# Operands of the first gate and up products split early, kept in DRAM and read back, in a one-core decoder trunk on Trainium2

## The chip, the cores and the metric

The kernel runs on 1 core of one Trainium2 chip. The metric is the device time of one execution in microseconds, taken as the median of 3 runs: 1397.15 us for the kernel before (1396.82 to 1398.56).

## The reference, cut to what matters

One layer (DEPTH = 1) over 1040 rows (1024 tokens behind 16 learned ones) of width 1024, in float32:

```python
u = rmsnorm(h, mix_norm_pre)
q, f_logit, i_in, g_out, v_pool, gate_a, gate_b = split(u @ w_in)
a = hgrn2(q, f_logit, i_in, g_out, ...)        # recurrence over chunks of 64 rows, 4 heads
p = multiscale_pool(v_pool, pool_proj, pool_scale)
z = sigmoid(gate_a) * (a @ w_branch_hgrn) + sigmoid(gate_b) * (p @ w_branch_pool)
h = h + rmsnorm(z @ w_out, mix_norm_post)
u = rmsnorm(h, ffn_norm_pre)
gt = causal_dwconv(u @ ffn_w_gate, conv_w, conv_b)          # 1024 -> 2816, three taps
y = (gelu(gt) * (u @ ffn_w_up)) @ ffn_w_down                # 2816 -> 1024
h = h + rmsnorm(y, ffn_norm_post)                           # returned without the 16 rows
```

## The kernel before

**Split products.** A float32 operand goes through TensorE as two parts of type fp32r. ScalarE (ACT) casts the raw tile `wraw` to its high part `whi`, and `wlo = wraw - whi` is the low part; each is a tile of 128 partitions x 1024 floats, 512 KB. A product is the sum of three chains of matmuls: high weights by high data, high by low, low by high (lines 262, 263 and 265 in a Strassen product, 160 to 162 and 172 to 174 elsewhere). `wsplit` (line 131) loads and splits one weight tile. Its subtraction stands on VectorE (DVE), or on GpSimd (POOL) for the tiles named in the table `POOLED`. `wraw`, `whi` and `wlo` have 3 buffers each, shared by all stages.

**Strassen units.** The gates of the mixer and the gate and up products of the MLP run as Strassen units of 256 output columns: seven products P1, P2, P6, P5, P3, P7, P4 instead of eight (class `Strassen`, line 179). P1, P2 and P4 take a block of the weights; P6, P5, P3 and P7 take sums of blocks, which POOL makes (lines 235 to 238). `ahead` (line 199) casts the operand on ACT (line 209) and subtracts on DVE (line 210), on POOL for the products 4 to 7 of the order. The data side is also split: P1 multiplies the quarter `b11` (tile `v`) of the normed rows, P2 `b21`, P3 `b22`, and P6, P5, P7 and P4 multiply sums of quarters, `t2`, `t1`, `t3` and `t4`. `put` adds a finished product in PSUM into the output (line 1197).

**The stages** in the order of time: values and pooling columns; the gate columns g; the mixer's gates, eight Strassen units that are each finished in two halves (100 to 262 us, the object `gates`); the stage that the string `ORDER` lists by hand (262 to 600 us): projections F (forget gates), Q, G, PV and PP by 128 columns each, among the steps `h0` to `h3` of the four heads, then the branch products BA and BB. A scheduler places the instructions there. Then the mix with `w_out` in three chunks of rows (600 to 716 us), and the **seam** from the mix to the MLP (716 to 796 us): the last chunk's three tiles of rows are added to the residual, normed (`own.norm`, lines 1106 to 1120), transposed on TensorE (line 1043) and combined into the quarters and their sums (`to_quarters`, lines 1046 to 1079). Eight products need only the first half of the rows, which was ready: P1 and P2 of gate units 0 to 3 (`EARLY` = 4). They stand among the transposes; the rest of gate unit 0 and then the whole of up unit 0 follow. From there on gate and up units alternate to 1196 us, and the down product ends the kernel.

In the seam and the mix the order of PE, ACT, DVE and POOL is the order of the code. SyncE (SP) issues loads and stores, in an order of its own; each waits for its buffer and for what it stores, and those behind wait with it.

**Names used below:** `tt` is a temporary of `to_quarters`; `un` a normed tile; `m` a tile of residual rows; `g` and `p` outputs and half sums of units; `pt` the transposes' bank; `swa`, `swb` the block sums; `st` a head's state; `d` and `kd` tables of a head.

Of the kernel before, what the change touches and what calls it, by code (L numbers as in the profile page):

```python
# [14 lines left out]
P = 128  # L15
# [19 lines left out]
HT = 514  # L35
# [8 lines left out]
ORDER = ("F0 c0 Q0 h0 F1 h0 c1 Q1 h0 h1 F2 h1 c2 h0 Q2 h1 h2 G2 h0 h1 h2 h0 F3 h0 h2 c3 PV0 h1 h2 h1 Q3 h3 h1 "  # L44
         "h3 h1 PV1 h3 sp0 PV2 h2 h3 sa1 sp1 sp2 PP0 h2 PV3 h2 h3 sp3 PP1 h0 G3 h3 PP2 h3 PP3 BB0 h2 BB1 BB2 "
         "sa2 BB3 h3 BB4 BB5 sa0 sa3 BA0 BA1 BB6 BA2 BB7 BA3 BA4 BA5 BA6 BA7")
# [10 lines left out]
def trunk_kernel(ctx: ExitStack, tc: tile.TileContext, x, meta_tokens, mix_norm_pre,  # L57
# [122 lines left out]
    class Strassen:  # L180
# [7 lines left out]
        def __init__(self, units, run, early, quarters, span, put, whole):  # L188
# [8 lines left out]
            self.got, self.at, self.prompt = [], 0, []  # L197

        def ahead(self, n):

            while len(self.got) < min(len(self.seq), self.at + n):
                i = len(self.got)
                if i % 2 == 0:
                    self.hi = wst.tile([P, 1024], F32R, tag="whi", name=nm("whi"))
                    self.lo = wst.tile([P, 1024], F32R, tag="wlo", name=nm("wlo"))
# [42 lines left out]
        def product(self, u, p, then=None):  # L248

            assert self.seq[self.at] == (u, p)  # L250
            x = pair(p)
# [4 lines left out]
            cuts = [(c0, o0, 512 - o0), (c0 + 512 - o0, 512, n - 512 + o0)][: 1 + (n + o0 > 512)]  # L256
            for k in range(4):
# [3 lines left out]
                for c, o, w in cuts:  # L261
                    pe.matmul(x[:, o : o + w], whi[:, k, :], xh[:, c : c + w], start=(k == 0), stop=False)  # L262
                    pe.matmul(x[:, o : o + w], whi[:, k, :], xl[:, c : c + w], start=False, stop=False)  # L263
                for c, o, w in cuts:
                    pe.matmul(x[:, o : o + w], wlo[:, k, :], xh[:, c : c + w], start=False, stop=(k == 3))  # L265
            x = x[:, o0 : o0 + n]
            if then and self.prompt:
                then(x)
                self.ahead(self.prompt.pop(0) - self.at)
                return x  # L270
            self.ahead(4)
            if then:
                then(x)
            return x
# [14 lines left out]
        def first(self, u):  # L289
# [3 lines left out]
            return (lambda: self.product(u, "P1", lambda x: act.copy(self.p1s[u], x)),  # L293
                    lambda: self.product(u, "P2", lambda x: self.put(u, 0, 0, self.p1s[u], x)))
# [7 lines left out]
        def rest(self, u):  # L302
            u2 = self.p1s[u]
            dve.tensor_tensor(u2, u2, self.product(u, "P6"), ALU.add)
            x5 = self.product(u, "P5")
            self.put(u, 0, 1, u2, x5, self.product(u, "P3"))
            self.whole(u, 0)
# [1190 lines left out]
```

## Time and profile before

| | us |
|---|---|
| median of 3 runs | 1397.15 |
| the profiled execution | 1396.61 |
| its span, first to last instruction | 1394.9 |
| PE busy | 1353.6 |
| DVE busy | 973.9 |
| ACT busy | 565.0 |
| POOL busy | 508.4 |

Some 1.7 us of the profiled execution lie outside the span. A stretch of the span is read with a row of the windows view: its length, the busy time of PE, PEld (weight loads), DVE, ACT and POOL, then the clock that TensorE was granted (1.00 is full), the share of the DMA engines and GB/s. The waits view lists idle time of an engine by the line that waited and the instruction that released it. Rows of the timeline give the start and the duration of one instruction or of a run of equal ones.

### The profile page before, as it was taken

What the parts mean: (1) busy time and instruction counts of PE and PEld (TensorE: products, weight loads), DVE (VectorE), ACT (ScalarE), POOL (GpSimd) and SP (SyncE); (2) the same over time, 40 slices, a digit from 0 to 9 for tenths busy, and PEclk for the clock granted to TensorE, in tenths of its full rate; (3) what the DMA queues carried; (4) which work ended last, traced back from release to release, by engine and by line L of the source; (5) the groups of instructions that cost most, each with busy time, mean ns of one, the idle gap of its engine ahead of it and who ended that gap; (6) DMA issues with size and microseconds to landing.
All of it is one profiled execution on the core that took longest, in us unless ns stands there. A gap on an engine that the chain in (4) does not pass through costs nothing. (4 is left out here: it accounts for less than half of the span.)

```text
span 1394.9 us, 21573 instructions
## 1 busy us (share of the span) xinstructions
PE 1353.6 (97%) x8405; PEld 1224.6 (88%) x8405; DVE 973.9 (70%) x1381; ACT 565.0 (41%) x945; POOL 508.4 (36%) x379
## 2 busy tenths in 40 slices
PE   8989999999999999999997999999999999999997
PEld 6879999999999899987777788888999988788786
DVE  6694655288975756565579888888887777654557
ACT  5443333356465463126564322222323223543343
POOL 4255331217543611051036565634567552000100
PEclk9999999999999999999998999999999999999999
DMA  6033433321111023589852577665677879966524
GB/s 245 31 100 121 138 104 108 103 73 46 33 33 33 18 76 122 182 265 316 288 172 91 148 218 214 192 173 145 161 166 188 197 194 268 365 231 201 179 71 166
DMA packets 133220, 215.21 MB, mean 154 GB/s; under 512 B 8327, under 2 KB 76523, under 8 KB 133120
## 3 DMA queue, kind: packets, MB, share of 16 engines
q1 hardware_dynamic: 121056, 189.47, 40.2%
q0 software_dynamic: 12064, 24.38, 10.3%
q8 instruction: 66, 1.08, 0.3%
q14 instruction: 34, 0.28, 0.1%
HBM read 160.84 MB, written 76.05 MB: 170 GB/s over the span
## 5 line engine op out<-in xcount | busy, mean ns | idle before, releaser
L262 PE MATMUL P<-v,whi 128*128 128x258 f32 (+2 forms) x528 | 162.6, 322 | 3.5 <-DVE g L1197 2.5
L263 PE MATMUL P<-v,whi 128*128 128x258 f32 (+2 forms) x528 | 161.6, 320 | 0.0
L265 PE MATMUL P<-v,wlo 128*128 128x258 f32 (+2 forms) x528 | 140.8, 321 | 1.1 <-DVE wlo L210 1.1
L137 POOL TENSOR_TENSOR wlo<-wraw,whi 128x1024 fp32r<-128x1024 f32 (+2 forms) x23 | 50.0, 2174 | 183.0 <-ACT whi L136 101.3
L262 PEld LDWEIGHTS P<-v,whi 128*128 128x128 f32 x528 | 100.8, 191 | 11.8 <-DVE g L1197 2.9
L263 PEld LDWEIGHTS P<-v,whi 128*128 128x128 f32 x528 | 100.7, 191 | 7.5
L161 PE MATMUL pd<-rot 128*128 128x512 f32 x272 | 106.0, 390 | 0.3 <-DVE rot L1257 0.3
L162 PE MATMUL pd<-rot 128*128 128x512 f32 x272 | 105.9, 389 | 0.0
L265 PEld LDWEIGHTS P<-v,wlo 128*128 128x128 f32 x528 | 87.9, 190 | 8.8 <-DVE wlo L210 1.3
L136 ACT CAST whi<-wraw 128x1024 fp32r<-128x1024 f32 (+2 forms) x44 | 36.2, 825 | 146.0 <-PE pba L174 31.3
L209 ACT CAST whi<-wraw 128x512 fp32r<-128x512 f32 x90 | 53.0, 617 | 101.8 <-PE P L263 83.9
L1257 DVE TENSOR_TENSOR rot<-yt,rot 128x1024 fp32r<-128x1024 f32 x33 | 41.2, 1250 | 71.0 <-ACT rot L1256 71.0
L210 DVE TENSOR_TENSOR wlo<-wraw,whi 128x512 fp32r<-128x512 f32 x82 | 75.9, 949 | 18.5 <-ACT whi L209 18.5
L1141 POOL TENSOR_TENSOR ys<-y 128x512 f32<-128x512 f32 x22 | 35.2, 1600 | 142.3 <-issue 96.8
L235 POOL TENSOR_TENSOR swa<-wraw,wraw 128x512 f32<-128x512 f32 x30 | 45.5, 1518 | 95.9 <-DMA wraw<-in_w_in_dram 62.4
L160 PE MATMUL pd<-rot 128*128 128x512 f32 x272 | 72.7, 390 | 2.0 <-ACT rot L1256 2.0
L1256 ACT CAST rot<-yt 128x1024 fp32r<-128x1024 f32 x33 | 34.6, 1053 | 90.2 <-PE pd L161 90.2
L209 ACT CAST whi<-swa 128x512 fp32r<-128x512 f32 x60 | 35.9, 619 | 86.8 <-PE P L263 71.6
L1189 DVE SCALAR_TENSOR_TENSOR y<-g,par,y 128x1024 f32<-128x1024 f32 x44 | 65.1, 1479 | 0.7
L160 PEld LDWEIGHTS pd<-rot 128*128 128x128 f32 x272 | 50.9, 188 | 13.5 <-ACT rot L1256 2.9
L210 DVE TENSOR_TENSOR wlo<-swb,whi 128x512 fp32r<-128x512 f32 x60 | 55.6, 932 | 9.7 <-ACT whi L209 9.4
L209 ACT CAST whi<-swb 128x512 fp32r<-128x512 f32 x60 | 35.9, 618 | 62.9 <-PE P L263 62.0
(344 smaller groups left out, 4320.2 us busy)
## 6 DMA issues: line engine op xcount, KB each, us to landing
wraw<-in_w_in_dram SPq DMA_DIRECT2D x36, 512.0 KB
yt<-ysum SPq DMA_DIRECT2D x33, 512.0 KB
wraw<-in_ffn_w_gate_dram SPq DMA_DIRECT2D x26, 512.0 KB
wraw<-in_w_out_dram SPq DMA_DIRECT2D x24, 512.0 KB
wraw<-in_ffn_w_up_dram SPq DMA_DIRECT2D x22, 512.0 KB
wsum<-in_ffn_w_down_dram SPq DMA_DIRECT2D x22, 512.0 KB
ysum<-ys SPq DMA_DIRECT2D x11, 768.0 KB
sa<-sscr SPq DMA_DIRECT2D x16, 513.0 KB
```

The lines of the kernel that those rows point to most:

```text
L137: eng.tensor_tensor(lo, raw, rr(hi), ALU.subtract)
L160: pe.matmul(ps, ahi, bhi, start=first, stop=False)
L161: pe.matmul(ps, ahi, blo, start=False, stop=False)
L162: pe.matmul(ps, alo, bhi, start=False, stop=last)
L209: act.copy(hi, src)
L210: (pool_e if 4 <= i < 2 * self.early else dve).tensor_tensor(lo, src, rr(hi), ALU.subtract)
L235: pool_e.tensor_tensor(s1, a21, a22, ALU.add)
L262: pe.matmul(x[:, o : o + w], whi[:, k, :], xh[:, c : c + w], start=(k == 0), stop=False)
L263: pe.matmul(x[:, o : o + w], whi[:, k, :], xl[:, c : c + w], start=False, stop=False)
L265: pe.matmul(x[:, o : o + w], wlo[:, k, :], xh[:, c : c + w], start=False, stop=(k == 3))
L1189: dve.scalar_tensor_tensor(a, g[:, :, j : j + n], cvw[:, j, m : m + 1], a, ALU.mult, ALU.add)
L1257: dve.tensor_tensor(lo, src, rr(hi), ALU.subtract)
```

## The change

Five things, all of one idea: operands that do not depend on data are split earlier, while PE works on the mixer's gates or on `ORDER`, and what was made lies in DRAM until it is wanted.

1. **Beside the gates.** After each half unit, `keep_next` runs one of 16 jobs: 12 make the low part of a weight tile of F, Q or PV (load, cast, subtraction, store of the low part), 4 split P1's and P2's operands of gate units 0 to 3 and store both parts. The stores are issued at the next call (`pay`).
2. **In `ORDER`.** The 12 loads of F, Q and PV read the raw tile and the kept low part (`wload`), and no longer subtract. Seven new steps `w4` and `w5` make the remaining five operands of gate unit 0 and the seven of up unit 0 (`keep_unit`), block sums included, on DVE and ACT, and store them.
3. **The first 20 products** of the MLP read ten pairs of kept tiles: no raw loads, block sums, casts or subtractions for them. Three tags of buffers take the pairs, and `lead` = 3 instead of `prompt` says how far ahead they are loaded.
4. **P2 onto P1.** `second` accumulates P2 in the bank in which P1's sum still stands, and ACT copies it to the output; before, `put` added it on DVE.
5. **The seam by hand.** `to_quarters` returns six steps, and the code calls them one by one among the products. The last chunk's `b22`, `t4` and `negdiff` go to DVE (argument `eng`); they stood on POOL.

The core of the diff:

```diff
-ORDER = ("F0 c0 Q0 h0 F1 h0 c1 Q1 h0 h1 F2 h1 c2 h0 Q2 h1 h2 G2 h0 h1 h2 h0 F3 h0 h2 c3 PV0 h1 h2 h1 Q3 h3 h1 "
+ORDER = ("F0 c0 Q0 h0 F1 h0 c1 Q1 h0 h1 F2 w4 h1 c2 h0 Q2 w4 h1 h2 G2 w4 h0 h1 h2 h0 F3 w5 h0 h2 c3 PV0 w5 h1 h2 h1 "
...
+                if i % 2 == 0 and i // 2 < len(self.kept):
+                    parts_, tags = self.kept[i // 2]
+                    both = [wst.tile([P, 1024], F32R, tag=t, name=nm(t), bufs=NRAW) for t in tags]
+                    for t, src in zip(both, parts_):
+                        self.loaded = nc.sync.dma_start(rr(t), src)
...
+            x = pair(p) if onto is None else onto
...
+    def keep(*what):
+        tiles_ = [wst.tile([P, 1024], F32R, tag=t, name=nm(t)) for t in ("whi", "wlo")]
...
+            if isinstance(src, tuple):
+                for a, op, b in src:
+                    dve.tensor_tensor(rr(lo), rr(lo) if a is None else a, rr(lo) if b is None else b, op)
+                src = rr(lo)
+            act.copy(hi, src)
+            dve.tensor_tensor(lo, src, rr(hi), ALU.subtract)
...
+    def keep_job(kind, i):
+        raw = wraw_tile()
+        nc.sync.dma_start(raw.rearrange("p (k c) -> p k c", k=KD), job(kind, i)[0])
+        hi, lo = (wst.tile([P, 1024], F32R, tag=t, name=nm(t)) for t in ("whi", "wlo"))
+        act.copy(hi, raw)
+        dve.tensor_tensor(lo, raw, rr(hi), ALU.subtract)
+        kept_w[kind, i] = dram.tile([P, 1024], F32, name=f"kept{kind}{i}")
+        owed.append((kept_w[kind, i], rr(lo)))
+
+    def wload(*key):
...
+        nc.sync.dma_start(rr(lo), kept_w[key])
+        act.copy(hi, raw)
...
+    def keep_next(u, i):
+        pay()
+        if beside:
+            beside.pop(0)()
...
-        put("b22", c22, d, pool_e)
-        put("t3", c12, d, dve)
-        negdiff(t2, t2, "b21", d)
-        return lambda: put("t4", t2, d, pool_e)
+        return [first_sums, lambda: put("t1", t1, d, dve), lambda: put("b22", c22, d, eng), difference,
+                lambda: negdiff(eng, t2, t2, "b21", d), lambda: put("t4", t2, d, eng)]
...
-        ffn.prompt = [5, 6, 8, 8, 8, 10, 10, 11]
...
+        ffn.lead, ffn.whole_pair = 3, True
...
+        todo.append(own.feat(0, dve))
+        second(0)
+        do(0)
...
+        first(3)
+        do(2)
+        do(1, 2)
+        second(2)
...
+        ffn.rest(RUN[0], dict(P6=[lambda: do(2, 3)]))
```

DVE in the seam, before: the queue from the last `un` on (L1120), with the sums of the three row tiles (`tt`; L1073, L1061, L1063) and the additions of finished P2s (`g`).

```order
L1120 SCALAR_TENSOR_TENSOR un_7222<-m_1008_7133,rstd_7226,g_790_6121 114x1024
L1197 TENSOR_TENSOR g_7254<-p_1015_7146,P_1031_7229 128x514
L1073 TENSOR_TENSOR tt_1041_7281<-tt_1043_7282,v_787_6117 128x456
L1073 TENSOR_TENSOR tt_1041_7281<-tt_1041_7281,v_787_6117 128x456
L1061 TENSOR_TENSOR tt_1041_7281<-tt_1043_7282,tt_1041_7281 128x456
L334 TENSOR_TENSOR t2l_6931<-tt_1041_7281,t2h_6929 128x2x114
L334 TENSOR_TENSOR t2l_6932<-tt_1041_7281,t2h_6930 128x2x114
L1063 TENSOR_TENSOR tt_1043_7282<-tt_1043_7282 128x456
L334 TENSOR_TENSOR v_788_6118<-tt_1041_7281,v_788_6118 128x4x114
L334 TENSOR_TENSOR t3l_6935<-tt_1043_7282,t3h_6933 128x2x114
L334 TENSOR_TENSOR t3l_6936<-tt_1043_7282,t3h_6934 128x2x114
L1197 TENSOR_TENSOR g_7328<-p_1015_7146,P_1044_7303 128x514
```

DVE at the same place now (the new L1232 is the old L1120, L1185 the old L1073, L1172 the old L1061, L348 the old L334):

```order
L1232 SCALAR_TENSOR_TENSOR un_7455<-m_1073_7377,rstd_7459,g_856_6365 114x1024
L1185 TENSOR_TENSOR tt_1094_7471<-tt_1096_7472,v_853_6361 128x456
L1185 TENSOR_TENSOR tt_1094_7471<-tt_1094_7471,v_853_6361 128x456
L1172 TENSOR_TENSOR tt_1094_7471<-tt_1096_7472,tt_1094_7471 128x456
L348 TENSOR_TENSOR t2l_7175<-tt_1094_7471,t2h_7173 128x2x114
L348 TENSOR_TENSOR t2l_7176<-tt_1094_7471,t2h_7174 128x2x114
L1185 TENSOR_TENSOR tt_1100_7517<-tt_1102_7518,v_853_6361 128x456
L1185 TENSOR_TENSOR tt_1100_7517<-tt_1100_7517,v_853_6361 128x456
L1172 TENSOR_TENSOR tt_1100_7517<-tt_1102_7518,tt_1100_7517 128x456
L348 TENSOR_TENSOR t2l_7175<-tt_1100_7517,t2h_7173 128x2x114
L348 TENSOR_TENSOR t2l_7176<-tt_1100_7517,t2h_7174 128x2x114
L348 TENSOR_TENSOR v_854_6362<-tt_1094_7471,v_854_6362 128x4x114
```

The additions into `g` are gone, and `t2` of the second row tile stands ahead of the first tile's `v`, `t1` and `t3`.

DVE in `ORDER`, after the tables `d` of head 1: before, one step follows the other there (L566 and L657 belong to the heads).

```order
L565 TENSOR_TENSOR d_3701<-d_3701,q_3636 128x130x4
L566 TENSOR_TENSOR d_3701<-d_3701,kk_3432 128x130x4
L657 COPY_PREDICATED sc_3023<-mbase,sb_3809 128x128 x4
L657 COPY_PREDICATED sc_3023<-mbase,sb_3818 128x128 x4
L660 COPY_PREDICATED scm_3024<-mbase,sm_3827 16x16
```

Now (the old L565 is L579, the old L657 is L671), with block sums (L845) and subtractions (L848) of step `w4` among them:

```order
L579 TENSOR_TENSOR d_3892<-d_3892,q_3815 128x130x4
L580 TENSOR_TENSOR d_3892<-d_3892,kk_3596 128x130x4
L845 TENSOR_TENSOR wlo_3820<-wraw_3606,wraw_3608 128x512
L845 TENSOR_TENSOR wlo_3820<-wraw_3606 128x512
L845 TENSOR_TENSOR wlo_3820<-wlo_3820,wraw_3606 128x512
L671 COPY_PREDICATED sc_3187<-mbase,sb_4006 128x128 x3
L845 TENSOR_TENSOR wlo_3820<-wraw_3608,wlo_3820 128x512
L671 COPY_PREDICATED sc_3187<-mbase,sb_4006 128x128
L671 COPY_PREDICATED sc_3187<-mbase,sb_4015 128x128 x4
L674 COPY_PREDICATED scm_3188<-mbase,sm_4024 16x16
```

Four block sums of 512 elements have come in between a head's tables and its selections.

SP in the gates, before: raw halves of the Strassen operands (L228) and stores of finished gates (`sscr`) alternate.

```order
L228 DMA wraw_1262<-in_w_in_dram 128x4x256
L777 DMA sscr<-sg_1224 128x514
L228 DMA wraw_1426<-in_w_in_dram 128x4x256
L777 DMA sscr<-sg_1255 128x514
L228 DMA wraw_1428<-in_w_in_dram 128x4x256
L779 DMA sscr<-sg_1356 128x512
```

Now, with the jobs' raw tiles (L896, 128x8x128) and the stores of what was kept (L862):

```order
L236 DMA wraw_1282<-in_w_in_dram 128x4x256
L791 DMA sscr<-sg_1244 128x514
L896 DMA wraw_1381<-in_w_in_dram 128x8x128
L791 DMA sscr<-sg_1275 128x514
L896 DMA wraw_1454<-in_w_in_dram 128x8x128
L793 DMA sscr<-sg_1376 128x512
L793 DMA sscr<-sg_1416 128x512
L862 DMA keptF_1387<-wlo_1384 128x1024
L236 DMA wraw_1461<-in_w_in_dram 128x4x256
L791 DMA sscr<-sg_1449 128x514
L236 DMA wraw_1463<-in_w_in_dram 128x4x256
```

Two jobs' raw tiles now stand ahead of the next unit's two halves in the three buffers of `wraw`, and a store of a low part ahead of them in the queue.

More of the change, by code (lines that the diff above doesn't have):

```diff
@@ L1273, in trunk_kernel @@
     last, t4s = None, []
+    assert ffn.seq[: len(KEPT)] == KEPT
+    ffn.kept = list(zip(kept, (("wraw", "wraw"), ("wraw", "wlo")) + (("whi", "wlo"),) * len(KEPT)))
     load_rows(0)
@@ L1304, in trunk_kernel @@
                 last = own
[L1306 to L1308 removed]
+        ffn.ahead(2)
         ws = [wo.next() for _ in range(3)]
```

195 lines of the change are left out of this document (133 added, 62 removed).

## The prediction

> **What bounds the kernel now.** I read the page's head first, then the windows by stage.
>
> ```profile
> PE 1353.6 (97%) x8405; PEld 1224.6 (88%) x8405; DVE 973.9 (70%) x1381; ACT 565.0 (41%) x945; POOL 508.4 (36%) x379
> 100.00:262.00 162.00, 159.63 (x1341) 159.63 (x1342) 80.73 (x115) 56.62 (x103) 55.66 (x41) 1.00 0.35 116
> 350.00:382.00 32.00, 30.68 (x251) 29.60 (x250) 31.89 (x70) 16.00 (x26) 18.01 (x7) 1.00 0.12 36
> 450.00:482.00 32.00, 29.50 (x226) 28.62 (x225) 28.91 (x38) 13.82 (x25) 18.94 (x8) 0.95 0.04 12
> 600.00:716.00 116.00, 112.85 (x526) 87.27 (x525) 70.57 (x91) 61.72 (x115) 27.29 (x23) 1.00 0.83 283
> 716.00:796.00 80.00, 65.99 (x423) 60.05 (x422) 71.68 (x85) 35.72 (x76) 46.10 (x37) 0.91 0.39 115
> 796.00:1196.00 400.00, 400.00 (x2473) 359.61 (x2471) 324.10 (x383) 116.80 (x181) 213.59 (x161) 1.00 0.75 197
> ```
>
> TensorE is busy for 1353.6 of 1394.9 us, so nothing is won except where it waits or runs slowly. One stage stands out: the seam, 716 to 796 us, with 14.0 us of idle PE, a clock of 0.91 and DVE busy for 71.68 of 80 us. The gates (100 to 262) have a full PE and a DVE half empty. In ORDER there are two stretches, 350 to 382 and 450 to 482, in which DVE is as good as full and PE already waits a little. After the seam PE is full for 400 us: what the seam gives is carried to the end.
>
> Next the waits of PE from 700 to 800, then the clock inside the seam:
>
> ```profile
> PE pt L1043 <- DVE g L1197: 6.2, 1, 6.2
> PE P L262 <- DVE g L1197: 2.9, 3, 1.8
> PE P L262 <- ACT t2h L333: 2.5, 1, 2.5
> PE P L265 <- DVE wlo L210: 1.1, 1, 1.1
> PE P L262 <- DVE p L308: 1.0, 1, 1.0
> 736.00:744.00 8.00, 1.80 (x14) 1.60 (x14) 8.00 (x7) 1.97 (x5) 7.89 (x6) 0.71 0.54 176
> 744.00:756.00 12.00, 9.53 (x60) 9.32 (x58) 10.89 (x15) 6.08 (x15) 4.93 (x4) 0.77 0.12 44
> 756.00:764.00 8.00, 7.91 (x51) 7.72 (x52) 7.98 (x11) 4.01 (x10) 6.32 (x5) 0.79 0.00 0
> ```
>
> DVE ends every large wait, directly or through the ACT cast of `t2h`. A mean clock of 0.71 over 8 us is 4.6 us at half, 0.77 over 12 is 5.5, 0.79 over 8 is 3.4: 13.5 us at half clock in all, of which some 4 us fall into the 6.2-us wait itself, so about 4.7 us of work are lost.
>
> How much is there at most? The first matmul of the seam, and the first of the second gate unit's P6, which ends it:
>
> ```profile
> 716.14 0.28 PE L262 MATMUL P<-v,whi 128*128 128x258 f32 x1
> L262 PE MATMUL P<-t2h,whi x8: 278/283/290, 796.0 to 798.4; 128*128 128x258 f32 x4, 128*128 128x256 f32 x4
> L265 PE MATMUL P<-t2h,wlo x8: 280/282/286, 796.4 to 798.7; 128*128 128x258 f32 x4, 128*128 128x256 f32 x4
> 787.61 0.39 PE L262 MATMUL P<-v,whi 128*128 128x512 f32 x1
> 790.39 0.40 PE L262 MATMUL P<-t3h,whi 128*128 128x512 f32 x1
> L1043 PE MATMUL pt<-ident,un 114*128 114x114 f32 x24 | 3.7, 308 | 6.2 <-DVE g L1197 6.2
> ```
>
> A gate product has 24 matmuls, the first at 796.0 and the last at 798.7: with one more start interval, 2.86 us. An up product (12 wide matmuls) starts 2.78 us after the one before it. Thirteen gate products, 24 transposes (at 0.1 us a start, 2.4 us) and seven up products are 37.2 + 2.4 + 19.5 = 59.1 us of work, and the stretch takes 79.8. **20.7 us** are lost there: 14.0 waiting, 4.7 by the clock, 2 at restarts. This is the ceiling of the change.
>
> **The seam, part by part.** What goes, and what the queue of DVE holds:
>
> ```profile
> L210 DVE TENSOR_TENSOR wlo<-wraw,whi 128x512 fp32r<-128x512 f32 x8 | 8.6, 1104 | 0.0
> L210 DVE TENSOR_TENSOR wlo<-swa,whi 128x512 fp32r<-128x512 f32 x6 | 6.1, 1030 | 0.1
> L1197 DVE TENSOR_TENSOR g<-p,P 128x514 f32<-128x514 f32 x7 | 4.7, 680 | 0.1
> 709.93 0.63 DVE L1063 TENSOR_TENSOR tt<-tt 128x456 f32<-128x456 f32 x1
> 710.47 0.63 DVE L334 TENSOR_TENSOR v<-tt,v 128x456 fp32r<-128x456 f32 x1
> 729.49 1.29 DVE L1120 SCALAR_TENSOR_TENSOR un<-m,rstd,g 114x1024 f32<-114x1024 f32 x1
> 736.96 1.69 DVE L1063 TENSOR_TENSOR tt<-tt 128x456 f32<-128x456 f32 x1
> ```
>
> Gone from DVE's queue are some 14 subtractions at 1.03 to 1.10 us and four additions at 0.68: about 17 of 71.7 us. Gone from POOL are the block sums of two units. Line 1063 stands there twice, the same operation: 0.63 us with POOL silent, 1.69 beside POOL's block sums. The moved `b22`, `t4` and `negdiff` put five 456-wide operations for each of three row tiles on DVE, at 0.54 us from start to start (709.93 to 710.47): 8 us. With POOL silent the operations that stay lose their extra 1.06 us, so DVE comes out well ahead.
>
> The new path: the order puts the eight early products and the three transposes one behind the other, 716.1 + 22.9 + 2.4 = 741.4 us for P6 of gate unit 0. P6 needs `t2` of the third row tile. The last `un` ended at 730.8 before; with the subtractions gone from among the norms I put its end at 728.7, an estimate. From there 19 operations at 0.54 us (two halves counted as one) stand to that `t2`: 10.3 us, and with 2 to 3 for their ACT casts 741 to 742. PE and DVE meet within half a microsecond, so 0.3 us of wait. P5, P3, P7 and P4 then have their data. Up's P1 needs the bank that P5's sum leaves, and its last addition stands on DVE behind three convolution operations of 1024 elements. Before, waits of this kind took 2.9 us in all and 1.8 at most; I take 2.6, between 0 and 5. With 0.3 for small ones: 20.7 − 3.2 = **17.5 us gained**, between 12 (one wait of 5 with its half clock) and 20.7.
>
> Whether 2.6 us idle also cost clock is read from a wait in ORDER:
>
> ```profile
> PE ppv L173 <- ACT st L667: 2.5, 1, 2.5
> 476.00:480.00 4.00, 2.94 (x10) 2.94 (x11) 4.00 (x7) 1.06 (x3) 0.00 (x0) 0.57 0.12 36
> 102.37 0.39 PE L262 MATMUL P<-uhi,whi 128*128 128x258 f32 x1 [2.66 <-ACT sg L714]
> 98.00:104.00 6.00, 3.34 (x24) 3.06 (x24) 4.51 (x15) 3.56 (x12) 3.73 (x5) 1.00 0.12 43
> ```
>
> A wait of 2.5 us was followed by 3.4 us at half clock, one of 2.66 us by none. So a wait of this length may cost 1.7 us more; that is in the range, not in the sum. The Trainium skill ("TensorE: Matmul & The Clock Gate", Part 1) has half rate only after an idle window of about 3.4 us: by it the sum stays at 1383.1, by the first row it would be 1384.8. The trace does not follow it in one of two cases.
>
> The ten pairs are 10.5 MB. A pair of 1.05 MB, at the 283 GB/s that the mix moved, takes 3.7 us, and two products take 5.7; loads go out two pairs ahead, so I cost them at nothing, with PE's products as cover. In SP's queue they stand behind the stores of residual rows, which wait for DVE until about 728; the pair behind them is wanted at 741.
>
> **Beside the gates.** Twelve jobs with one cast and one subtraction of 1024, four with two of each of 512, are some 20 us on DVE and 17 on ACT (prices below), where 81 and 105 us are free. Loads and stores add 18.9 MB in 162 us, 117 GB/s to 116; 283 was carried elsewhere. What it does cost is look-ahead: jobs take turns in the three `wraw`, so a unit's second raw half waits for the subtraction of the unit before. By the order, units 2 and 3 get P6's operands with under 1 us to spare, later ones with about 5. I take 1 us, between 0 and 6. Reading F's first low part back at the entry of ORDER passes SP's stores: 0.5 us, between 0 and 3.
>
> **In ORDER.** The rows for both sides, the same operation twice for each of two cases, and the page's groups:
>
> ```profile
> 352.66 3.40 POOL L137 TENSOR_TENSOR wlo<-wraw,whi 128x1024 fp32r<-128x1024 f32 x1
> 353.72 3.44 DVE L626 TENSOR_TENSOR kd<-kd,kk 128x1040 f32<-128x1040 f32 x1
> 373.80 1.23 DVE L626 TENSOR_TENSOR kd<-kd,kk 128x1040 f32<-128x1040 f32 x1
> 362.21 2.86 DVE L565 TENSOR_TENSOR d<-d,q 128x520 f32<-128x520 f32 x1
> 365.60 0.69 DVE L565 TENSOR_TENSOR d<-d,q 128x520 f32<-128x520 f32 x1
> 366.21 0.69 DVE L566 TENSOR_TENSOR d<-d,kk 128x520 f32<-128x520 f32 x1
> L136 ACT CAST whi<-wraw 128x1024 fp32r<-128x1024 f32 (+2 forms) x44 | 36.2, 825 | 146.0 <-PE pba L174 31.3
> 470.98 3.48 DVE L137 TENSOR_TENSOR wlo<-wraw,whi 128x1024 fp32r<-128x1024 f32 x1
> ```
>
> Seven steps add 26 operations of 512 on DVE, 0.61 us each (365.60 to 366.21): 15.9 us. Ten subtractions leave POOL. About 13 of the 26 fall into 350 to 382: +7.9 us, against 2.2 each for two operations that no longer run beside POOL's subtractions: +3.5 net in a stretch where PE has 1.3 us of idle. About 9 fall into 450 to 482: +5.5, but there the subtraction of 3.48 us that stands ahead of the state update (`st`, PE's 2.5-us wait) comes later in the new order. Together I take 2 us, between −4 (that wait and its half clock gone) and 8 (nothing hidden).
>
> **The sum.** −17.5 + 1 + 0.5 + 2 = −14.0 from the profiled 1396.61, 1382.6; the median stands 0.5 above the profiled execution, so **1383.1 us**.
>
> **The rivals.**
> - *DVE stays the bound of the seam.* For: 0.5 us decide at P6. If six of its operations run beside POOL or wait for ACT as at 736.96, P6 is 6.5 us late and loses 1.7 by the clock: gain 9.3, net −5.8, 1391.3. Against: POOL has no block sums before P6 in the new order. 0.15.
> - *Slower: the added DVE work starves PE in ORDER.* If the 22 operations in the two full stretches run at 1.69 us each, as beside POOL's heads' work, they are 37 us, of which the relief (4.4), PE's idle time there (3.8) and the subtraction that moves (3.5) cover 12: 25 us, and net −17.5 + 1.5 + 25 = +9, 1406. It turns the sign from 1.27 us an operation on. Against: POOL loses 10 subtractions. 0.14.
> - *Gates starve.* Eight units each late by 2 us: 16, net about 0 to +2, 1398. Against: about 5 us of slack in the later units. 0.05.
> - *Kept pairs arrive late.* SP's queue is in order; six pairs each 2 us late give 12 back: 1395. 0.06.
>
> **The numbers.** The forecast has 0.60. About 0.2% (2.8 us) is what a measurement can tell from no change. Faster: 0.60 + 0.15 + half of the last rival, 0.78; same: half of each of the last two, 0.06; slower: 0.14 and the rest, 0.16. The low end is a seam at its ceiling with gains in ORDER: 1374. The high end takes in the first and last rival: 1396.
>
> **What would show it.** Right: from the first P1 of the seam to the second gate unit's P6 about 62 us instead of 79.8, no 6.2-us wait at the transposes, a clock near 1.00, the largest wait at up's P1; PE in 100 to 262 idle for at most 4 us. Wrong: new waits of PE on `wlo` or on loads in the gates, DVE full from 350 to 382 with PE idle for over 4 us, or a wait at P6 of several microseconds.

## The result: 4.8 us slower, and the profile after

The changed kernel takes 1402.36 us (median of 20 runs, 1398.23 to 1406.59) against 1397.56 of the kernel before on the same chips: a ratio of 1.0034, 95% interval 1.0023 to 1.0045. The forecast was 1383.1, with 1396 as the end of its range. The profiled execution shown here took 1406.11 us, so it lies 3.7 us above the median, and the stages below add up to more than the medians differ by.

First the head of the changed kernel's page:

```profile
span 1404.3 us, 21770 instructions
...
PE 1356.8 (97%) x8405; PEld 1226.7 (87%) x8405; DVE 980.7 (70%) x1420; ACT 579.0 (41%) x961; POOL 455.8 (32%) x342
```

PE is busy for 3 us more in a span that is 9.4 us longer. The windows of the changed kernel follow (columns as before: PE, PEld, DVE, ACT, POOL busy, granted clock, DMA share, GB/s): the gates, the seam, which lies 23 us later here, and three windows around single waits.

```profile
100.00:262.00 162.00, 155.00 (x1277) 154.80 (x1278) 92.31 (x127) 68.64 (x116) 53.32 (x39) 0.98 0.64 202
739.00:805.00 66.00, 61.88 (x426) 57.06 (x425) 52.96 (x81) 28.16 (x63) 14.99 (x11) 0.97 0.71 237
167.00:181.00 14.00, 8.83 (x52) 8.63 (x51) 7.15 (x9) 5.62 (x9) 5.34 (x4) 0.76 0.76 233
269.00:285.00 16.00, 11.87 (x60) 11.13 (x59) 0.69 (x1) 4.49 (x6) 0.00 (x0) 0.79 1.03 329
482.00:494.00 12.00, 8.41 (x36) 7.54 (x36) 11.92 (x20) 8.41 (x12) 6.47 (x3) 0.72 0.46 158
```

The waits of PE in the changed kernel:

```profile
PE P L272 <- ACT whi L217: 5.2, 1, 5.2
PE ppp L173 <- DVE sc L671: 3.6, 1, 3.6
...
PE pq L173 <- ACT whi L908: 3.0, 1, 3.0
PE P L272 <- DVE p L321: 2.5, 1, 2.5
...
PE sm L673 <- ACT sg L728: 1.4, 1, 1.4
...
PE pf L173 <- ACT whi L908: 1.1, 1, 1.1
PE sb L668 <- DVE sc L615: 1.1, 1, 1.1
```

The 6.2-us wait of the seam is gone. Three new places took its room: one wait of 5.2 us in the gates, 3.0 and 1.1 at the entry of `ORDER`, and several inside it. The waits of 5.2, 3.0 and 3.6 us were each followed by half clock: means of 0.76 over 14 us, 0.79 over 16 and 0.72 over 12 in the last three windows are 6.7 us at half in each.

Where the lengths of stages come from, in the changed kernel: two rows of the timeline, the first product of the gates and of the seam,

```profile
101.83 0.39 PE L272 MATMUL P<-uhi,whi 128*128 128x258 f32 x1 [3.39 <-ACT sg L728]
...
738.89 0.28 PE L272 MATMUL P<-v,wraw 128*128 128x258 f32 x1
```

and the groups of F's, BB's and the second gate unit's P6's first chain, with the times of the first and the last:

```profile
L173 PE MATMUL pf<-uhi,whi x96: 316/322/658, 270.0 to 402.2; 128*128 128x346 f32 x64, 128*128 128x348 f32 x32
L173 PE MATMUL pbb<-phi,whi x96: 313/320/580, 534.2 to 599.4; 128*128 128x342 f32 x96
...
L272 PE MATMUL P<-t2h,whi x8: 277/283/287, 804.5 to 806.9; 128*128 128x258 f32 x4, 128*128 128x256 f32 x4
```

So the gates took 168.1 us from their first product, F to BB0 264.3, the seam 65.6 from its first product to P6. Before, read in the same way: 160.0, 250.5 and 79.8. The table has this in us for every kernel run (their names are explained with the experiments), each from one profiled execution, beside the median and the ratio of its runs to those of before on the same chip. What one execution can differ by is seen where code is the same: the gates of after, jobs_unused, w_late, w_act, w_thin and w_slot took 167.0 to 171.0 us, and ORDER took 264.3 in after and 270.1 in own_lo, 259.9 in jobs_unused and 265.5 in thin_store. Much of that is the clock. These two windows begin behind the same waits at `sb`, the first in jobs_unused, the second in thin_store:

```profile
373.00:390.00 17.00, 13.44 (x136) 12.37 (x135) 16.93 (x30) 13.16 (x22) 4.68 (x2) 1.00 0.39 137
...
375.00:392.00 17.00, 16.25 (x111) 15.15 (x112) 16.93 (x29) 13.21 (x22) 4.66 (x2) 0.50 0.39 133
```

In thin_store PE ran for 17 us at half clock there, in jobs_unused not at all, though the two waits before were 0.9 and 1.1 us in the one and 0.8 and 1.1 in the other. So a stage of one execution is better compared by PE's idle time, its length less PE's busy time, beside its length.

| kernel | gates | F to BB0 | BB0 to mix | mix | seam | median | ratio (95%) |
|---|---|---|---|---|---|---|---|
| before | 160.0 | 250.5 | 94.2 | 109.2 | 79.8 | 1397.6 | |
| after | 168.1 | 264.3 | 94.8 | 109.8 | 65.6 | 1402.4 | 1.0034 (1.0023 to 1.0045) |
| no_jobs | 168.8 | 259.2 | 94.8 | 112.0 | 62.1 | 1399.3 | 1.0017 (1.0006 to 1.0028) |
| own_lo | 163.6 | 270.1 | 94.8 | 109.0 | 62.6 | 1397.3 | 1.0006 (0.9991 to 1.0021) |
| first_first | 173.0 | 255.5 | 94.9 | 113.7 | 62.6 | 1399.8 | 1.0027 (1.0010 to 1.0043) |
| jobs_unused | 167.9 | 259.9 | 94.9 | 109.0 | 62.0 | 1397.8 | 1.0010 (0.9992 to 1.0027) |
| thin_store | 166.7 | 265.5 | 94.9 | 110.2 | 62.9 | 1399.2 | 1.0018 (1.0005 to 1.0031) |
| w_late | 169.7 | 250.0 | 101.5 | 110.5 | 62.9 | 1398.1 | 1.0005 (0.9992 to 1.0018) |
| w_act | 167.0 | 269.1 | 95.6 | 109.2 | 62.5 | 1402.9 | 1.0043 (1.0029 to 1.0057) |
| w_thin | 169.2 | 254.4 | 94.2 | 111.2 | 62.7 | 1394.8 | 0.9979 (0.9964 to 0.9993) |
| w_slot | 171.0 | 281.8 | 94.1 | 109.8 | 62.2 | 1423.6 | 1.0186 (1.0169 to 1.0204) |
| late | 160.0 | 250.5 | 108.8 | 109.7 | 62.8 | 1394.8 | 0.9978 (0.9968 to 0.9988) |
| late_u | 161.5 | 250.4 | 107.6 | 110.1 | 62.4 | 1394.6 | 0.9977 (0.9968 to 0.9986) |
| seam_pool | 160.0 | 249.9 | 108.6 | 109.2 | 62.5 | 1393.8 | 0.9973 (0.9964 to 0.9983) |
| mid_u | 160.1 | 248.3 | 99.8 | 109.7 | 63.0 | 1385.8 | 0.9926 (0.9912 to 0.9939) |
| mid_u2 | 162.7 | 249.8 | 99.7 | 111.1 | 62.1 | 1388.0 | 0.9933 (0.9919 to 0.9946) |

### The profile page after: what moved, and what is told of

Its sections match the earlier page's. It is cut to its first block, busy times and chain, and to the rows that moved or that the text cites. A ratio compares the mean times of both kernels' runs of the same rounds, so it can differ in the third digit from the quotient of the medians.

```text
span 1404.3 us, 21770 instructions
## 1 busy us (share of the span) xinstructions
PE 1356.8 (97%) x8405; PEld 1226.7 (87%) x8405; DVE 980.7 (70%) x1420; ACT 579.0 (41%) x961; POOL 455.8 (32%) x342
## 5 line engine op out<-in xcount | busy, mean ns | idle before, releaser
L272 PE MATMUL P<-v,whi 128*128 128x258 f32 (+1 forms) x496 | 153.6, 323 | 4.1 <-DVE p L321 2.5
L273 PE MATMUL P<-v,whi 128*128 128x258 f32 (+1 forms) x496 | 153.2, 323 | 0.0
L275 PE MATMUL P<-v,wlo 128*128 128x256 f32 (+2 forms) x512 | 137.6, 322 | 0.0
L272 PEld LDWEIGHTS P<-v,whi 128*128 128x128 f32 x496 | 94.1, 190 | 12.8 <-DVE p L321 2.9
L273 PEld LDWEIGHTS P<-v,whi 128*128 128x128 f32 x496 | 94.0, 190 | 7.8
L275 PEld LDWEIGHTS P<-v,wlo 128*128 128x128 f32 x512 | 85.0, 189 | 7.7
L217 ACT CAST whi<-wraw 128x512 fp32r<-128x512 f32 x78 | 46.1, 618 | 97.0 <-PE P L273 80.0
L218 DVE TENSOR_TENSOR wlo<-swa,whi 128x512 fp32r<-128x512 f32 x56 | 51.2, 923 | 20.2 <-ACT whi L217 6.7
L160 PEld LDWEIGHTS pd<-rot 128*128 128x128 f32 x272 | 50.8, 188 | 14.0 <-ACT rot L1369 2.3
L272 PE MATMUL P<-t2h,whi 128*128 128x258 f32 (+1 forms) x196 | 57.4, 310 | 5.2 <-ACT whi L217 5.2
L161 PEld LDWEIGHTS pd<-rot 128*128 128x128 f32 x272 | 51.1, 188 | 11.3 <-DVE rot L1370 0.7
L162 PEld LDWEIGHTS pd<-rot 128*128 128x128 f32 x272 | 51.1, 188 | 10.6
```

The costliest lines, as they stand in the source:

```text
L160: pe.matmul(ps, ahi, bhi, start=first, stop=False)
L161: pe.matmul(ps, ahi, blo, start=False, stop=False)
L162: pe.matmul(ps, alo, bhi, start=False, stop=last)
L217: act.copy(hi, src)
L218: (pool_e if 4 <= i < 2 * self.early else dve).tensor_tensor(lo, src, rr(hi), ALU.subtract)
L272: pe.matmul(d, whi[:, k, :], xh[:, c : c + w], start=(k == 0 and onto is None), stop=False, **go)
```

## The experiments

### Where the gates lose

Without the twelve jobs for F, Q and PV (`no_jobs`; the four jobs of the MLP then take the first four half units):

```diff
-    beside = [lambda o=o_: keep_job(*o) for o_ in order if o_[0] in ("F", "Q", "PV")]
-    beside += [lambda e=e: keep_first(e) for e in range(EARLY)]
+    beside = [lambda e=e: keep_first(e) for e in range(EARLY)]
```

> The changed kernel without the twelve jobs for F, Q and PV beside the gates; ORDER loads and splits these tiles as before, and the steps w4 and w5 stay in ORDER. Theory A (tiles that are held until their stores have landed, and raw loads queued behind them, starve PE in the gates and at the entry of ORDER): the gates take 160 to 161 us again from their first product to F's first matmul (168.1 in the changed kernel), the waits on whi at F and Q go, and the time is 1402.4 - 8 - 7 = about 1387 us. Theory B (the work that was added on DVE inside ORDER is the loss): the gates hardly change what the end sees, and with POOL's subtractions back the stage F to BB0 is longer than the changed kernel's 264 us; about 1402 or more.

Measured 1399.3 us. The entry's waits went, as theory A had it, but the gates' wait stayed, at 5.5 us: a miss. So the number and the kind of the jobs do not explain it: the four cost as much here as all sixteen did.

Low parts of the twelve jobs in buffers of their own (`own_lo`):

```diff
-        hi, lo = (wst.tile([P, 1024], F32R, tag=t, name=nm(t)) for t in ("whi", "wlo"))
+        hi, lo = wst.tile([P, 1024], F32R, tag="whi", name=nm("whi")), slot(1024, F32R, "klo")
```

> The changed kernel, but the low parts that the twelve jobs make lie in buffers of their own instead of the three of wlo. Theory A: the wait of 5.2 us in the gates (a subtraction that waited for a low part's store to land) goes with its half clock, gates 160 to 162 us; at the entry the buffers of the last four jobs are still held, so its 7 us stay: about 1394. Rival (the raw loads are late by the DMA traffic itself, not by the buffers): gates remain at 166 to 168 us, about 1402.

Measured 1397.3, not 1394. The wait fell to 1.8 us and the gates to 163.6; the entry's loss stayed. What the low parts' buffers did to this stays open: in this execution PE also ran at half clock from 102.9 us on (0.61 over 102 to 106), so it came to unit 3 later, and P6 started there 69.2 us after the gates' first product, where the six profiled executions with the changed kernel's gates have 68.4 to 71.6; the 163.6 itself lies below their 167.0 to 171.0. Last, whole stores against stores of 8 columns, with ORDER splitting for itself in both (`jobs_unused`, `thin_store`):

```diff
-    loader = Loader([o_ if o_ in kept_w else job(*o_)[:2] + (P, eng("w%s%d" % o_)) for o_ in order if o_[0].isupper()],
+    loader = Loader([job(*o_)[:2] + (P, eng("w%s%d" % o_)) for o_ in order if o_[0].isupper()],
...
-        owed.append((kept_w[kind, i], rr(lo)))
+        owed.append((kept_w[kind, i], rr(lo)[:, :8]))      # thin_store alone
```

> The changed kernel with its sixteen jobs beside the gates, but ORDER splits F, Q and PV itself as before and reads no kept low part. Gates as in the changed kernel, 167 to 173 us with a wait of 3 to 5 us in the third unit. Reading the low parts back should be worth 1 to 4 us in ORDER, so F to BB0 is 1 to 4 us longer here than the changed kernel's 264.3: 1403 to 1406.

> As the kernel whose low parts are made and not used, but the twelve jobs store 8 columns of the low part instead of 1024. If low parts held until their stores have landed are the gates' loss, the wait in the third unit falls below 1 us and the gates take 160 to 163 us; the total falls by 5 to 8 against the kernel with whole stores. If the raw tiles that the jobs load (a third of wraw, and ahead of the unit's own halves in SP's queue) are the loss, the gates stay at 167 us or more.

The wait on `whi` was 2.5 us with whole stores and 1.2 with thin ones, but the gates took 167.9 and 166.7 us: other waits, on `sg` and `p`, took the room (2.5 us with whole stores, 3.7 with thin ones). The total did not fall, and the first expectation, 1403 to 1406, was missed from below; why is told with the entry. So the landing of the low parts' stores is at most a small part. The trace shows the larger one: when POOL starts the block sums of the mixer's units 2 and 3 (unit 3 is the one that my expectations call the third). POOL's timeline before:

```profile
134.47 1.29 POOL L235 TENSOR_TENSOR swa<-wraw,wraw 128x512 f32<-128x512 f32 x1 [5.27 <-DMA wraw<-in_w_in_dram]
...
147.59 1.31 POOL L235 TENSOR_TENSOR swa<-wraw,wraw 128x512 f32<-128x512 f32 x1 [7.62 <-DMA wraw<-in_w_in_dram]
```

The same two in the changed kernel:

```profile
147.85 1.29 POOL L243 TENSOR_TENSOR swa<-wraw,wraw 128x512 f32<-128x512 f32 x1 [19.30 <-DMA wraw<-in_w_in_dram]
...
167.40 1.29 POOL L243 TENSOR_TENSOR swa<-wraw,wraw 128x512 f32<-128x512 f32 x1 [13.92 <-DMA wraw<-in_w_in_dram]
```

And in `mid_u`, a kernel told of below, in which no job stands in the early half units:

```profile
131.97 1.30 POOL L242 TENSOR_TENSOR swa<-wraw,wraw 128x512 f32<-128x512 f32 x1 [3.87 <-DMA wraw<-in_w_in_dram]
...
146.09 1.32 POOL L242 TENSOR_TENSOR swa<-wraw,wraw 128x512 f32<-128x512 f32 x1 [8.94 <-DMA wraw<-in_w_in_dram]
```

Units 2 and 3 had their sums started at 134.5 and 147.6 us before, at 147.9 and 167.4 after, and unit 3's P6 was due at 167.8. The queue of SP in the changed kernel says why:

```profile
127.46 0.37 SPq L896 DMA_DIRECT2D wraw<-in_w_in_dram  x1
128.55 0.38 SPq L896 DMA_DIRECT2D wraw<-in_w_in_dram  x1
...
139.43 0.41 SPq L236 DMA_DIRECT2D wraw<-in_w_in_dram  x1
...
156.22 0.41 SPq L236 DMA_DIRECT2D wraw<-in_w_in_dram  x1
...
162.81 0.38 SPq L236 DMA_DIRECT2D wraw<-in_w_in_dram  x1
163.24 0.50 SPq L862 DMA_DIRECT2D keptQ<-wlo  x1
```

And DVE's timeline:

```profile
170.05 1.63 DVE L218 TENSOR_TENSOR wlo<-swa,whi 128x512 fp32r<-128x512 f32 x1 [4.49 <-DMA keptQ<-wlo]
```

The two buffers that came free at 127 us went to jobs (L896), where before unit 2's halves stood. The look-ahead fell back by a whole unit and never came back: unit 3's second half left at 162.81, and POOL could start at 167.40. At the same time DVE waited 4.5 us for `keptQ`, 6.8 us after its issue. That is not what PE's wait of 5.2 us ended with: P6 began at 172.96, behind the cast of its sum on ACT, and ACT's timeline shows what stood ahead of that cast.

```profile
171.34 1.04 ACT L898 CAST whi<-wraw 128x1024 fp32r<-128x1024 f32 x1 [1.46 <-DMA wraw<-in_w_in_dram]
172.29 0.61 ACT L217 CAST whi<-swa 128x512 fp32r<-128x512 f32 x1
```

POOL had the sum ready at 171.1; ACT was waiting for a job's raw tile and then cast it first, which cost 1.2 us more. That the place is what counts is shown by `no_jobs` and `mid_u`: the same four jobs cost 8.8 us in the first four half units (gates 168.8) and 0.1 us from the sixth on (160.1; 162.7 in `mid_u2` with the same gates, 161.5 in `late_u` without any job there).

### Where the entry of ORDER loses

In the changed kernel the last jobs store both parts. ACT's timeline at the entry, with what its casts for F and Q waited for:

```profile
272.98 1.04 ACT L908 CAST whi<-wraw 128x1024 fp32r<-128x1024 f32 x1 [2.65 <-DMA kept3h<-whi]
...
276.04 1.04 ACT L908 CAST whi<-wraw 128x1024 fp32r<-128x1024 f32 x1 [1.48 <-DMA wraw<-in_w_in_dram]
```

The first of the two stood behind the store of `kept3h`, which still held its `whi`. `first_first` turns the order of the jobs round:

```diff
-    beside = [lambda o=o_: keep_job(*o) for o_ in order if o_[0] in ("F", "Q", "PV")]
-    beside += [lambda e=e: keep_first(e) for e in range(EARLY)]
+    beside = [lambda e=e: keep_first(e) for e in range(EARLY)]
+    beside += [lambda o=o_: keep_job(*o) for o_ in order if o_[0] in ("F", "Q", "PV")]
```

> The changed kernel with the sixteen jobs beside the gates in another order: the four that store both parts come first, the twelve of F, Q and PV after them. If F's cast at the entry of ORDER waited for a high part whose store had not landed (the last job before it stored both), the waits of 3.0 and 1.1 us at pq and pf go, and from F's first matmul to BB0 it takes 257 to 259 us instead of 264.3: 1395 to 1397 in all. If any job at the end of the gates does this, it stays at 262 to 265. The wait of 5 us in the third gate unit should stay, as it did without the twelve jobs.

F to BB0 took 255.5 us, without a wait at `pq` or `pf`: the entry is settled. The total, 1399.8, missed its 1395 to 1397: the gates took 173.0 with the wait of 5.4 us, and the mix 113.7. The same numbers say what the kept low parts are worth: 255.5 with them, 259.2 and 259.9 where ORDER subtracted for itself with the same steps `w4`, `w5` and no wait on casts at the entry (`no_jobs`, `jobs_unused`). That is some 4 us, of which 2.1 and 2.8 are idle PE (7.0 against 9.1 and 9.8) and the rest clock. (`thin_store`, with the same ORDER as these two, had 7.9 us of idle PE and its 17 us at half clock: 265.5.) The entry took back 7 us in the changed kernel's profiled execution, 4.1 of them waits; in `w_late` and `w_thin`, which have the same entry, it came down to 2.3 and 2.2 us of waits and no half clock. `jobs_unused`, which throws the jobs' work away and pays next to nothing of this, came out at 1397.8, below the changed kernel and against its expectation.

### Where ORDER loses

The steps `w4` and `w5` moved behind PP3, among BB and BA (`w_late`):

```diff
-... F2 w4 h1 c2 h0 Q2 w4 h1 h2 G2 w4 h0 h1 h2 h0 F3 w5 ... PV0 w5 ... PV1 w5 ... PV2 w5 ...
+... BB3 h3 w4 BB4 w4 BB5 w4 sa0 sa3 BA0 BA1 BB6 w5 BA2 w5 BB7 w5 BA3 w5 BA4 BA5 BA6 BA7
```

> The changed kernel with its seven steps w4 and w5 moved behind PP3, among BB and BA; the twelve jobs stay beside the gates. Theory A: only the 6.8 us that were lost inside ORDER after its entry can go, the gates keep their 168 us and the entry its 7 us: 1395 to 1397 us. Theory B: the same 6.8 us go, and nothing else is left to explain, so the time should fall below before's 1397.6 by most of the seam's 14 us: about 1384. A third case: the stalls inside ORDER come from low parts that are read back late; then they stay and the time remains near 1402.

F to BB0 fell to 250.0 us, the waits inside ORDER to those of before, and the gates kept their loss. The total came to 1398.1 and not 1395 to 1397, because BB0 to the mix grew to 101.5. So the loss inside ORDER comes with the steps; but is it the length of their operations, or the buffers that they wait for? Two kernels asked. In `w_act` ACT copies raw blocks into both parts, and DVE has none of the 26 operations, so the MLP's first products go without block sums and low parts:

```diff
-            if isinstance(src, tuple):
-                for a, op, b in src:
-                    dve.tensor_tensor(rr(lo), rr(lo) if a is None else a, rr(lo) if b is None else b, op)
-                src = rr(lo)
+            if at[0] >= 2 * EARLY:
+                src = src[0][0] if isinstance(src, tuple) else src
+                act.copy(hi, src)
+                act.copy(lo, src)
+                continue
```

> The changed kernel, but the seven steps w4 and w5 in ORDER make no sums and no subtractions: ACT copies a raw block into both parts (two casts where there was one, and 26 DVE operations less). The values of the MLP's first products are therefore not the reference's; its time is read for ORDER alone. Theory B (DVE's 26 operations delay the heads): from F's first matmul to BB0 the 264.3 us shrink by 7 to 9, and PE's waits between 370 and 385 us and the one of 3.6 us at ppp fall back to those of before (1.1 and 2.5 us); about 1394 us. Theory A (the buffers that the steps hold until their stores land): the stage stays at 262 to 265 us, about 1402.

In `w_thin` the 26 operations stay where they are in DVE's queue, 8 columns wide. The casts read raw blocks instead of the sums, and the high part is stored a second time in the low part's place:

```diff
-                    dve.tensor_tensor(rr(lo), rr(lo) if a is None else a, rr(lo) if b is None else b, op)
+                    dve.tensor_tensor(rr(lo)[:, :1, :8], a[:, :1, :8], b[:, :1, :8], op)
...
+                dve.tensor_tensor(lo[:, :1, :8], src[:, :1, :8], rr(hi)[:, :1, :8], ALU.subtract)
...
+            tiles_[1] = tiles_[0]
```

> The changed kernel, but the 26 operations that the steps w4 and w5 put on DVE work on 8 columns instead of 512, in the same places of the queue; the high part is stored in place of the low one and is a raw block, so the first MLP products are not the reference's. If the time of the DVE operations is ORDER's loss, F to BB0 shrinks from 264.3 to about 257 (7 us of entry wait stay), the waits at sb, sc and ppp fall to before's: 1395. If the waits for buffers in DVE's queue are the loss, it stays at 262 to 265: 1402.

PE's longest wait from F to BB0 in `w_act`:

```profile
PE ppv L173 <- ACT st L681: 6.5, 1, 6.5
```

And of `w_thin`:

```profile
PE ppv L173 <- ACT st L681: 2.7, 1, 2.7
PE pq L173 <- ACT whi L916: 1.4, 1, 1.4
```

`w_thin` answers it: the stage fell to 254.4 us, the waits at `sb` and `ppp` are gone (what is left is before's wait at `ppv`, the entry's and small ones), and 1394.8 us is what was expected of the operations' length. DVE's own waits for buffers stayed, as two rows of `w_thin` show,

```profile
433.60 0.24 DVE L846 TENSOR_TENSOR wlo<-wraw,wraw 128x8 f32<-128x8 f32 x2 [2.81 <-PE pq L177]
...
473.06 0.17 DVE L846 TENSOR_TENSOR wlo<-wraw,wraw 128x8 f32<-128x8 f32 x1 [2.29 <-PE ppv L177]
```

so they are not the loss. `w_act` alone would have misled. Its stage did not shrink (269.1): PE waited 6.5 us at `ppv <- ACT st`, for a head's state, and ACT had stood still before it:

```profile
497.27 1.05 ACT L767 CAST plh<-s 128x1026 fp32r<-128x1026 f32 x1 [6.88 <-DVE s L762]
```

What ACT waited for came from DVE, so the 12 further casts on ACT are not shown to be this delay; how the queues came to stand so stays open. This is how the delay looks on DVE in the changed kernel, at the 3.6-us wait of `ppp`:

```profile
477.31 0.69 DVE L845 TENSOR_TENSOR wlo<-wraw,wraw 128x512 f32<-128x512 f32 x1 [2.30 <-PE ppv L177]
...
478.53 2.40 DVE L845 TENSOR_TENSOR wlo<-wlo,wraw 128x512 f32<-128x512 f32 x1
480.85 0.49 DVE L671 COPY_PREDICATED sc<-mbase,sb 128x128 f32<-128x128 uint8 x2
481.25 2.00 DVE L845 TENSOR_TENSOR wlo<-wraw,wlo 128x512 f32<-128x512 f32 x1
483.18 2.39 DVE L848 TENSOR_TENSOR wlo<-wlo,whi 128x512 fp32r<-128x512 f32 x1
485.49 1.28 DVE L671 COPY_PREDICATED sc<-mbase,sb 128x128 f32<-128x128 uint8 x6
```

The last six selections of `sc`, which `ppp`'s matmuls stand behind, come 4.6 us after the first two (485.49 against 480.85), behind two of the steps' operations at 2.0 and 2.4 us, about three times the 0.69 of the first row. Before those DVE had also stood still for 2.3 us, on a buffer that a projection still used.

`w_slot` gave the steps slots of the general pool instead:

```diff
-        tiles_ = [wst.tile([P, 1024], F32R, tag=t, name=nm(t)) for t in ("whi", "wlo")]
+        tiles_ = [slot(1024, F32R, "khi"), slot(1024, F32R, "klo")]      # raw tiles likewise
```

> The changed kernel, but the steps w4 and w5 in ORDER work in slots of the general pool instead of wraw, whi and wlo; the same 26 operations on DVE at the same steps. If the buffers are what delays ORDER (DVE's queue stood still for 2.3 us at 477 us on a whi or wlo that a projection still used), F to BB0 shrinks from 264.3 to 256 to 259, entry wait included, and the 3.6-us wait at ppp falls to 2.5 or less; about 1396 us. If the operations themselves delay it, the stage stays at 262 us or more and the time near 1402.

It took 1423.6 us, and neither case holds: PE was idle for 5.5, 4.3 and 4.2 us on the heads' tiles `s`, `st` and `d`, which take slots of the same pool. That these tiles waited for slots is not shown. The run says nothing on the three small buffers.

### Everything behind ORDER

In `late` nothing stands beside the gates, F, Q and PV are split as before, and all operands of the 20 products are made among BB and BA (`beside = []`, steps `k0` to `k3` and `w4`, `w5` from BB0 to BA3).

> F, Q and PV split as before, nothing beside the gates, and all operands of the first 20 products made among BB and BA, where DVE was busy for 47 of 87 us. Theory A: gates and ORDER as before (160 and 250 us), the seam's 14 us kept, 1397.6 - 14 = 1383 to 1385 us. Rival: the three buffers of each kind starve BB and BA there just as they did the gates; the stretch from BB0 to the mix grows from 94 to 100 us or more, 1390 us or more.

Gates, ORDER and seam came out as theory A had them (160.0, 250.5, 62.8 us), but BB0 to the mix took 108.8 and the whole 1394.8 us, as the rival had it (100 or more, 1390 or more). `late_u` gives the steps the memory that the normed inputs leave free after G3:

```diff
-        tiles_ = [wst.tile([P, 1024], F32R, tag=t, name=nm(t)) for t in ("whi", "wlo")]
+        tiles_ = [sub("hi", F32R), sub("lo", F32R)]     # parts of two ubig tiles, raw tiles likewise
```

> As the kernel with everything made among BB and BA, but raw tiles and both parts lie in the memory that the normed inputs leave free after G3, not in the three buffers of wraw, whi and wlo. Theory A: BB and BA wait for their weights no longer, BB0 to the mix takes 94 to 97 us instead of 108.8, the seam keeps its 17 us: 1381 to 1384 us. Rival (the DMA traffic itself, 0.8 of the engines' time there, makes the weights late): 104 us or more, 1390 or more.

The largest waits of PE from BB0 to the mix in `late`:

```profile
PE pba L172 <- ACT whi L135: 4.5, 4, 1.9
PE pba L176 <- POOL wlo L136: 1.6, 1, 1.6
```

In `late_u`:

```profile
PE pbb L172 <- DVE sa L800: 7.5, 1, 7.5
```

The waits on weights went with the buffers, and one of 7.5 us came, which neither case had foreseen: BB's sums `sa` stood on DVE behind steps that the scheduler, with memory free, had put there all at once. The time was 1394.6 us, above the 1381 to 1384 of theory A. So the load had to be spread: `mid_u` makes the eight P1 and P2 operands beside the gates, but only after the 6th, 8th, 10th and 12th half unit, and the other twelve behind BB0 in the free memory.

```diff
+        calls.append(u)
+        if beside and len(calls) in (6, 8, 10, 12):
             beside.pop(0)()
```

> P1's and P2's operands of gate units 0 to 3 are made beside the gates, but only behind the 6th, 8th, 10th and 12th half unit; the other twelve among BB and BA in memory of their own; F, Q and PV as before. Theory A: the early half units were the place that had no buffer to spare, so the gates take 160 to 161 us, ORDER 250, BB0 to the mix 94 to 96, the seam 62.8: 1380 to 1383 us. If a job costs wherever it stands, the gates take 164 us or more: 1385 to 1389.

Four of its windows: the gates, the first part of ORDER, the end of ORDER behind G3, and the seam.

```profile
100.00:262.00 162.00, 161.06 (x1350) 161.00 (x1351) 85.97 (x119) 61.77 (x109) 56.69 (x39) 1.00 0.48 157
262.00:350.00 88.00, 88.00 (x633) 87.35 (x632) 66.72 (x133) 51.26 (x78) 36.89 (x18) 1.00 0.21 60
500.00:520.00 20.00, 17.46 (x111) 14.96 (x109) 13.26 (x25) 12.87 (x23) 1.52 (x1) 1.00 0.73 244
719.00:782.00 63.00, 59.92 (x422) 55.50 (x421) 52.30 (x80) 27.79 (x62) 14.53 (x11) 1.00 0.74 248
```

The gates are full again, the seam has no half clock, and 2.5 us are lost behind G3. It takes 1385.8 us, 0.74% under the kernel before (0.61 to 0.88%) and some 1.1% under the changed one: the version to keep. It is still 3 us above the expected 1380 to 1383, since BB0 to the mix took 99.8 us and not 94 to 96. `mid_u2` moves its seven steps to BB3 and later.

> The best version so far (1385.8 us) with its seven steps a little later, from BB3 on instead of right behind BB0, where heads 2 and 3 still ran and PE lost some 4 us (waits of 1.4 at po and 1.0 at ms). If that was their work in the queues of DVE, ACT and SP, BB0 to the mix takes 95 to 97 us instead of 99.8: 1382 to 1384 us. If the later place only moves the collision onto BB's and BA's weights, 99 us or more and no gain.

It took 1388.0 us, and BB0 to the mix the same 99.7: no gain, the second case of the expectation.

### What in the seam made the gain

`seam_pool` is `late` with the last chunk's `b22`, `negdiff` and `t4` on POOL again (`own.feat(i)` without `dve`).

> The kernel with everything made among BB and BA (1394.8 us, seam 62.8 us from its first product to the second gate unit's P6), but the last chunk's b22, negdiff and t4 stand on POOL again. By the prediction's reading of the seam (an operation on DVE takes three times as long beside POOL) t2 of the third row tile and with it P6 come later: seam 65 to 70 us, 1397 to 1402. If the kept operands and the order of the products alone make the gain, the seam stays within 1 us: 1394 to 1396.

Its window of the seam:

```profile
730.00:793.00 63.00, 60.64 (x426) 55.98 (x425) 52.59 (x66) 28.21 (x63) 30.85 (x26) 1.00 0.75 252
```

The seam is as short, 62.5 us, with POOL busy for 30.9 us of it, twice as long as in `mid_u`. Moving those steps to DVE bought nothing; what is left is the kept operands, the order of products and sums, and P2 in P1's bank. These three were not taken apart.

## Why the prediction was wrong

**The seam was right.** 17.5 us were forecast from a ceiling of 20.7. Thirteen kernels with this seam needed 62.0 to 63.0 us against 79.8, a gain of 16.8 to 17.8; the changed kernel's profiled execution needed 65.6, with 2.5 us of wait at up's P1 (2.6 forecast) and half clock behind it. P6 waited for nothing, and no product waited for a kept pair, as costed. The 2.6 was luck in part: in the thirteen others up's P1 waited 0.4 to 1.5 us, and in all of them an early P1 waited 1.2 us for ACT's copy of an earlier P1's sum, a wait that the prediction did not name. One reason given for the gain, POOL's silence, was not needed (`seam_pool`).

**The step that failed is "what it does cost is look-ahead ... I take 1 us, between 0 and 6".** The place was named (P6's operands of unit 3 with under 1 us to spare) and its price was not: 5.2 us of wait and half clock behind it, 8.1 in all. Two jobs' tiles took the buffers that unit 2's halves were to have, so unit 2's sums began 13 us later and unit 3's 20 us later than before. The spare time was counted with every transfer on time, and no term stood for a job's cast ahead of P6's on ACT, nor for the clock.

**The entry, "0.5 us, between 0 and 3", measured 7 in the profiled execution**, 4.1 of it waits and the rest half clock. I followed the kept low part through SP's queue. What was late was a high part's cast, on a buffer that a store still held; that wait was on no list.

**ORDER, "2 us, between −4 and 8", measured 6.6 behind the entry**, inside its range but with the wrong value taken. The relief by subtractions that ORDER no longer makes was there (some 4 us by length, 2 to 3 by idle PE; 4.4 counted). What failed is the price of the added operations: `no_jobs` and `jobs_unused`, which have only the steps added there, need 8.7 and 9.4 us more than before, 5.3 and 6.0 of them idle PE, and `w_thin` takes 9.9 away, but nearly half of these at the entry, where it waited 1.9 us less and kept its clock. I had counted 13.4 us of them on DVE and let the moved subtraction and PE's slack take most of it. Together the 26 kept DVE busy for 30 us where 15.9 were counted: 18 ran at 0.7 us and eight at 1.8 to 2.9, with POOL busy for at least 0.7 of each of the eight. They stood ahead of the selections, and in place of the 2.5-us wait that the moved subtraction was to shorten came one of 3.6.

**The sum and the range.** Two terms were taken near their low ends and the third in the middle of its range, and the range as a whole let one go wrong at a time. In the profiled execution the terms are +8.1, +7 and +6.6 in place of 1, 0.5 and 2, and −14.2 in place of −17.5; with 1.2 us from BB0 to the seam they give +8.7 of the 9.5 us by which it is longer than the profiled execution before. The medians differ by 4.8 us: this execution shows the losses large. In others with the same code at the entry, for example, the waits there were 2.2 to 3.6 us and not 4.1. Of the 21.9 us lost before BB0 some 13.7 are waits and the rest half clock, for which the sum had no term there. The slower rival had the right mechanism for ORDER at 0.14, though it counted 25 us. "Gates starve", at 0.05, had the right place, but eight units late by 2 us where one was late by 5.2. They happened together, which had no chance of its own.

## What to carry to other kernels

Work put beside a full TensorE is free only if it takes no buffer from the stage's own look-ahead: ask which load is issued later because of it, and when its tile is wanted. A tile that is stored holds its buffer until the store has landed (here casts and subtractions stood still for 2.7 and 4.5 us on it), so such jobs belong away from the start of the next stage and spread out; memory of their own helps only where nothing else needs it. And operations added to an engine's queue cost their length wherever the next thing in it is waited for: with the same 26 operations 8 columns wide the waits behind them were gone.

## What the runs showed of the hardware that I had not expected

Whether a wait of PE costs half clock as well is not told by its length: in the changed kernel's profile a wait of 3.39 us (at 101.8) was followed by full clock, one of 2.5 us in the seam by half clock (0.97 over 66 us is some 4 us at half), and in thin_store two waits of 0.9 and 1.1 us by 17 us at half while PE was busy for 16.25 of them (the windows above the table). Over the 20 executions of the changed kernel, too, the time goes mostly with the granted clock: 0.988 to 0.993 in the six fastest, 0.985 to 0.989 in the six slowest. The window around the first of these waits:

```profile
98.00:106.00 8.00, 4.61 (x38) 4.33 (x37) 3.97 (x14) 4.55 (x14) 4.07 (x5) 1.00 0.19 72
```
